# Gathering a sample's compression rows in two halves, and compressing its keys and values side by side

## The chip, the cores and the metric

The kernel runs on one core of one Trainium2 chip. The time of a run is the device time of that core in microseconds (us), from one launch; the median of three runs is the figure that counts. An "engine" is one of the core's five instruction streams: PE (matrix multiply; its weight loads are listed apart as PEld), DVE (vector), ACT (scalar and activation), POOL (general, and here the issuer of indirect DMAs) and SP (which only issues DMAs).

## The reference, cut to what matters

One decoder layer is computed for two request groups: a prompt of 1024 tokens, and 8 samples of 8 new tokens each, with 2048 tokens of past in paged caches.

```
x = ffn_half(x, norm_ffn1, ffn1_wg, ffn1_wu, ffn1_wd)     # x + (silu(h@wg) * (h@wu)) @ wd / 2
q, kc, vc, ks, vs, kw, vw, gates, z, xbc, dtr = split_proj(rmsnorm(x) @ w_in)
o_att  = nsa_mixer(q, ...)      # compressed, selected and window attention
y_ssm  = mamba_mixer(z, xbc, ...)
x = x + concat(o_att, y_ssm) @ w_out
x = ffn_half(x, norm_ffn2, ffn2_wg, ffn2_wu, ffn2_wd)

def compress(rows, pe, w1, w2):            # once for K, once for V
    ch  = rows.reshape(b, T // 16, 16, KV_HEADS, HEAD_DIM)
    blk = concatenate([ch[:, :-1], ch[:, 1:]], axis=2) + pe      # blocks of 32 tokens, stride 16
    blk = blk.transpose(0, 1, 3, 2, 4).reshape(b, nc - 1, KV_HEADS, 32 * HEAD_DIM)
    return silu(blk @ w1) @ w2
```

The change touches `compress` for the samples' past only: for each of 8 samples, 128 chunks of 16 tokens are fetched from the paged cache and turned into 127 compressed keys and 127 compressed values for each of 2 KV heads.

## The kernel before, in words

All of the kernel is one program whose order on each engine is fixed when it is built (a scheduler works on a model of the engines and writes out one list per engine). The tokens, 1024 of the prompt and 64 of the samples, make 1088 columns, worked on as two halves of 544, each cut into pieces of 256 and of 288 columns (`SUBS`). Nearly every product in fp32 is made of three passes, a high part and a low part of each operand: weights-high times data-high, weights-low times data-high, weights-high times data-low. On the page these show as three lines one after another: L366, L367, L368 for gate and up of the feed-forward parts (outputs gX and gY), L412 to L414 for the first columns of it (output g), L633 to L635 for the down projection (output dq), L250 to L252 for the projections q, xbc, z. A weight load of 128x128 goes with each matmul.

The stages, in us from the span's start: gate and up of the first feed-forward part about 100 to 520, its down projection to 710, projections and Mamba to 1136, prompt attention to 1548, sample attention and output projection to 1760, gate and up of the second feed-forward part to 2170, its down projection to the end.

The moving operands of gate and up are the tiles B1 to B7 (`b_tiles`, L112), each of four k-slices of 256 or of 288 columns; the weights are `whi` and `wlo`. SBUF tiles come from stacked pools on two sides, "left" and "right" of the memory. The constants pool `C` (L214 for `idx`) is the first on the left, so its size sets where all later left-side tiles start. `b_tiles` puts filling tiles between the B tiles, so that these start at chosen bytes modulo 256 (`PLACE = (96, 160)`, L110).

In the attention stage the prompt's eight query tiles run one after another, and 3, 0, 2, 1, 1, 0, 1, 0 of the samples' compressions (`compress_sample`, L1702) are written ahead of them; the scheduler weaves the two together. One compression does this:

- one indirect DMA (`gather`, L1686, issued by POOL at L1689, with row numbers in `idx`) brings 128 chunks of 16 tokens into `chk`, one buffer of 16 KB per partition; the next gather can only be issued once every reader of that buffer is through,
- eight steps, four for K and then four for V. A step (`pairs`, L1704) copies 4 tokens' worth of rows into `chp` (half on ACT, half on POOL, L267), transposes it with four PE instructions into `cT` (L1712), and splits the result into `th` (ACT) and `tl` (DVE, L1717), of which there are two pairs. Twelve matmuls (L1733 to L1735) then add it to `cA` in PSUM; one step's `pairs` is written ahead of the step before's matmuls,
- after four steps, `cmp_hidden` (L1406) reads `cA` with ACT (L1410), and two small matmuls give the compressed keys, or values (`c2`).

`cA` is one PSUM buffer of half a bank, used by K, then by V, then by the next sample's K.

Of the kernel before, what the change touches and what calls it, by code (L numbers as in the profile page):

```python
# [10 lines left out]
F32 = mybir.dt.float32  # L11
F32R = mybir.dt.float32r
BF16 = mybir.dt.bfloat16
I32 = mybir.dt.int32
AF = mybir.ActivationFunctionType
OP = mybir.AluOpType
AX = mybir.AxisListType

P = 128
# [22 lines left out]
def f32(ap):  # L42
    return ap.bitcast(F32)
# [37 lines left out]
def hybrid_step(ctx: ExitStack, tc: tile.TileContext, *aps):  # L81
    nc = tc.nc
# [129 lines left out]
    w2 = C.tile([P, 2, 64], F32, name="w2")  # L212
    gd = C.tile([P, 9, 32], F32, name="gd")
    idx = C.tile([P, 8], I32, name="idx")  # L214


    def blocks(n):
# [48 lines left out]
    def copy(eng, out, src):  # L266
        return nc.scalar.copy(out, src) if eng == "a" else ENGINES[eng].tensor_copy(out, src)  # L267
# [448 lines left out]
    def late():  # L716
        at = 0
        for name, n in VECS:
            nc.sync.dma_start(vr[at:at + n], rows(A[name], n))
            at += n  # L720
        nc.sync.dma_start(w2[:, 0], A["cmp_w2_k"][0])
        nc.sync.dma_start(w2[:, 1], A["cmp_w2_v"][0])

        ptile = C.tile([P, 8], I32, name="ptile")
        pt = A["page_table"]
        for a in range(16):
            nc.sync.dma_start(ptile[8 * a:8 * a + 8], bass.AP(
                tensor=pt.tensor, offset=pt.offset + a, ap=[[0, 8], [16, 8]]))
        nc.vector.tensor_scalar(w2, w2, 0.5, None, op0=OP.mult)
        q = bankx("vec_ps")  # L730
        nc.tensor.transpose(q[:, :NV], vr, ident[:NV, :NV])
        nc.vector.tensor_copy(vec, q[:, :NV])
        lane = C.tile([P, 1], I32, name="lane")
        nc.gpsimd.iota(lane, pattern=[[0, 1]], base=0, channel_multiplier=1)
        nc.vector.tensor_scalar(lane, lane, 7, None, op0=OP.bitwise_and)
        lanef = C.tile([P, 1], F32, name="lanef")
        nc.vector.tensor_copy(lanef, lane)
        nc.vector.tensor_scalar(idx, ptile, 8.0, lanef, op0=OP.mult, op1=OP.add)

    def begin1():  # L740
        g = First(F1, w1g, silu_out, raw0)
# [932 lines left out]
    with pool("att", bufs=2) as K, pool("att_ps2", bufs=3, space=PSUM) as PS2, \  # L1674
# [3 lines left out]
            return PS1.tile([P, 512], F32, name=name, tag=tag, bufs=2 if name == "pT" else 1)  # L1678


        ch_cmp = A["cache_cmp"][0].rearrange("n (c s) k g d -> (n c) (s k g d)", s=16)
        with tc.issue_after(wload.ins):
            for b in range(8):
                nc.sync.dma_start(nwin_s[0, b, 0:504].rearrange("t k g d -> t (k g d)"),
                                  A["cache_win"][0, b, 8:512].rearrange("t k g d -> t (k g d)"))

        def gather(b):
            chk = CK.tile([P, 16, 2, 2, 64], F32, name="chk", bufs=1)
            nc.gpsimd.indirect_dma_start(  # L1689
                out=chk.rearrange("p s k g d -> p (s k g d)"), out_offset=None, in_=ch_cmp,  # L1690
                in_offset=bass.IndirectOffsetOnAxis(ap=idx[:, b:b + 1], axis=0))
            return chk

        first_chk = gather(0)

        tpad = []
        for i in range(2):
# [2 lines left out]
                nc.gpsimd.memset(f32(t[:, :, 256:]), 0.0)  # L1700

        def compress_sample(b):  # L1702
            chk = gather(b) if b else first_chk
            def pairs(kv, jj):  # L1704
                chp = CK.tile([P, 2, 2, 2, 64], F32, name="chp", bufs=1)
                for g in range(2):
                    copy(KN["chp"][g], chp[:, :, g], chk[:, 4 * jj:4 * jj + 4, kv, g, :].rearrange(
                        "p (j r) d -> p j r d", r=2))
                q = b1("cT")
                for u in range(2):  # L1710
                    for g in range(2):
                        nc.tensor.transpose(q[:, P * (2 * u + g):P * (2 * u + g) + P],  # L1712
                                            chp[:, u, g].rearrange("p r d -> p (r d)"), ident)
                sv = q.rearrange("p (u c) -> p u c", u=2)
                th, tl = tpad[jj % 2]
                copy(KN["th"][jj % 2], th[:, :, :256], sv)
                nc.vector.tensor_tensor(tl[:, :, :256], sv, f32(th[:, :, :256]), op=OP.subtract)  # L1717

            steps = [(kv, jj) for kv in range(2) for jj in range(4)]
            pairs(*steps[0])  # L1720
            for kv in range(2):
                ab = PSC.tile([P, 2, P], F32, name="cA")
                for jj in range(4):
                    if (kv, jj) != steps[-1]:
                        pairs(*steps[4 * kv + jj + 1])
                    th, tl = tpad[jj % 2]
                    for u in range(2):
                        j = 2 * jj + u
                        for z in range(2):
                            wh, wl = w1h[:, kv, 8 * z + j], w1l[:, kv, 8 * z + j]  # L1730
                            first = j == 0 and z == 0
                            mh, ml = (x[:, u, z:z + 256].rearrange("p (g c) -> p g c", g=2) for x in (th, tl))
                            nc.tensor.matmul(ab, wh, mh, start=first, stop=False, skip_group_check=True)  # L1733
                            nc.tensor.matmul(ab, wl, mh, start=False, stop=False, skip_group_check=True)
                            nc.tensor.matmul(ab, wh, ml, start=False, stop=(j == 7 and z == 1), skip_group_check=True)  # L1735
                hs = cmp_hidden(CK, ab[:, :, :127], None, kv, 127)
                q = b1("c2")
                for g in range(2):
                    if kv == 0:
# [793 lines left out]
```

## Time and profile before

| what | value |
|---|---|
| median of 3 runs | 2473.76 us (2468.87 to 2475.54) |
| the profiled execution's own time | 2475.45 us |
| its span, first to last instruction | 2473.8 us |
| mean granted TensorE clock | 0.987 |
| PE busy | 2408.8 us, 97% of the span |
| PE weight loads | 2222.8 us, 90% |
| DVE / ACT / POOL busy | 71% / 46% / 17% |
| bytes moved by DMA | 379.07 MB, mean 153 GB/s |

"Busy" adds up the time during which an engine has at least one instruction at work; consecutive matmuls overlap, so how long a matmul really takes of the engine is read from the distance between the starts of two of them, not from the length of one. "Idle before" is time in which an engine stood still ahead of an instruction, with the instruction that released it.

### The profile page before, as it was taken

What the parts mean: (1) busy time and instruction counts of PE and PEld (TensorE: products, weight loads), DVE (VectorE), ACT (ScalarE), POOL (GpSimd) and SP (SyncE); (2) the same over time, 40 slices, a digit from 0 to 9 for tenths busy, and PEclk for the clock granted to TensorE, in tenths of its full rate; (3) what the DMA queues carried; (4) which work ended last, traced back from release to release, by engine and by line L of the source; (5) the groups of instructions that cost most, each with busy time, mean ns of one, the idle gap of its engine ahead of it and who ended that gap; (6) DMA issues with size and microseconds to landing.
All of it is one profiled execution on the core that took longest, in us unless ns stands there. A gap on an engine that the chain in (4) does not pass through costs nothing.

```text
span 2473.8 us, 48193 instructions
## 1 busy us (share of the span) xinstructions
PE 2408.8 (97%) x19026; PEld 2222.8 (90%) x19026; DVE 1744.7 (71%) x3673; ACT 1131.2 (46%) x2501; POOL 418.3 (17%) x533
## 2 busy tenths in 40 slices
PE   7999999999999999999999999999999999999998
PEld 6999999999999998997667766677899999999998
DVE  6777776677778855655656666777967676768776
ACT  7544444441133254425666675444545454543113
POOL 0000000011134343333434343111000000001110
PEclk9999999999999999999999998999999999999999
DMA  4334343598652333423110104476235353559654
GB/s 162 134 133 160 130 164 129 175 338 306 230 190 84 126 116 102 119 69 127 40 64 35 69 35 148 130 250 213 89 123 171 120 174 120 174 213 370 238 209 153
DMA packets 230446, 379.07 MB, mean 153 GB/s; under 512 B 18509, under 2 KB 147705, under 8 KB 228812
## 3 DMA queue, kind: packets, MB, share of 16 engines
q1 hardware_dynamic: 210248, 318.02, 37.7%
q0 software_dynamic: 7600, 38.59, 4.5%
q10 hardware_dynamic: 12372, 19.38, 2.2%
q8 instruction: 150, 2.46, 0.4%
q14 instruction: 76, 0.62, 0.1%
HBM read 255.66 MB, written 124.40 MB: 154 GB/s over the span
## 4 chain that ended last, share of the span: by engine, by line
PE 86%; DVE 6%; DMA 4%; ACT 3%; issue 1%; POOL 0%; ACTq 0%; DVEq 0%; POOLq 0%
PE dq L634 6%; PE gY L367 6%; PE dq L633 6%; PE dq L635 6%; PE gY L368 6%; PE gY L366 6%; PE gX L367 5%; PE gX L366 5%; PE gX L368 5%; PE o L1855 3%; PE pT L1846 3%; PE s L1808 1%; PE xbc L250 1%; PE xbc L251 1%; PE xbc L252 1%; PE cA L1733 1%
## 5 line engine op out<-in xcount | busy, mean ns | idle before, releaser
L634 PE MATMUL dq<-db,da 128*128 128x256 f32 (+1 forms) x1232 | 353.2, 288 | 0.3 <-DVE da L270 0.3
L635 PE MATMUL dq<-db,da 128*128 128x256 f32 (+1 forms) x1232 | 352.8, 288 | 0.0
L633 PE MATMUL dq<-db,da 128*128 128x256 f32 (+1 forms) x1232 | 349.8, 288 | 2.7 <-DVE Cc L386 2.2
L642 DVE TENSOR_TENSOR xT<-xT,dq 128x256 f32<-128x256 f32 (+1 forms) x456 | 186.9, 432 | 84.8 <-PE dq L635 83.2
L270 POOL TENSOR_TENSOR ds<-dw 128x512 f32<-128x512 f32 x22 | 29.5, 1341 | 1228.1 <-DVE wlo L270 508.0
L633 PEld LDWEIGHTS dq<-db,da 128*128 128x128 f32 x1232 | 230.5, 189 | 3.3 <-DVE Cc L386 2.5
L635 PEld LDWEIGHTS dq<-db,da 128*128 128x128 f32 x1232 | 232.8, 189 | 0.0
L634 PEld LDWEIGHTS dq<-db,da 128*128 128x128 f32 x1232 | 231.9, 188 | 0.6 <-DVE da L270 0.5
L267 ACT CAST whi<-ws 128x512 fp32r<-128x512 f32 x156 | 96.5, 623 | 205.9 <-PE gY L368 137.6
L270 DVE TENSOR_TENSOR wlo<-raw,whi 128x512 fp32r<-128x512 f32 x184 | 125.5, 687 | 83.9 <-ACT whi L267 83.5
L267 ACT CAST da<-ds 128x512 fp32r<-128x512 f32 x88 | 52.6, 623 | 234.7 <-PE dq L635 93.4
L267 ACT CAST whi<-raw 128x512 fp32r<-128x512 f32 x181 | 112.4, 626 | 72.0 <-PE g L414 19.5
L270 DVE TENSOR_TENSOR wlo<-ws,whi 128x512 fp32r<-128x512 f32 x156 | 106.7, 687 | 42.4 <-ACT whi L267 41.9
L1824 ACT ACTIVATE pb<-s,mx 128x256 f32<-128x256 f32 (+3 forms) x192 | 105.0, 552 | 59.7 <-DVE mx L1822 37.6
L1846 PEld LDWEIGHTS pT<-ident,pb 128*128 128x128 f32 x528 | 59.6, 143 | 45.8 <-issue 40.1
L1821 DVE TENSOR_REDUCE mx<-s 128x1 f32<-128x384 f32 (+2 forms) x128 | 66.6, 536 | 44.0 <-PE s L1813 34.1
L366 PE MATMUL gY<-B3h,whi 128*128 128x256 f32 (+1 forms) x320 | 91.5, 287 | 1.5 <-ACT whi L267 1.4
L366 PE MATMUL gX<-B6h,whi 128*128 128x256 f32 (+1 forms) x320 | 91.3, 286 | 0.9 <-ACT Cc L373 0.9
L367 PE MATMUL gX<-B6h,wlo 128*128 128x256 f32 (+1 forms) x320 | 91.4, 286 | 0.6 <-DVE wlo L270 0.6
L367 PE MATMUL gY<-B3h,wlo 128*128 128x256 f32 (+1 forms) x320 | 91.6, 287 | 0.2 <-DVE wlo L270 0.2
L277 POOL TENSOR_TENSOR pb<-pb,sm 128x640 f32<-128x640 f32 (+7 forms) x70 | 85.1, 1238 | 37.6 <-DVE sm L1831 34.0
L367 PE MATMUL gY<-B2h,wlo 128*128 128x256 f32 (+1 forms) x320 | 91.4, 286 | 0.0
(763 smaller groups left out, 8548.1 us busy)
## 6 DMA issues: line engine op xcount, KB each, us to landing
db<-GD SPq DMA_DIRECT2D x42, 1632.0 KB
GD<-Cc SPq DMA_DIRECT2D x154, 272.0 KB
GD<-his SPq DMA_DIRECT2D x84, 272.0 KB
raw<-in_ffn_wu_dram SPq DMA_DIRECT2D x22, 1024.0 KB
dw<-in_ffn_wd_dram SPq DMA_DIRECT2D x44, 512.0 KB
raw<-in_ffn_wg_dram SPq DMA_DIRECT2D x21, 1024.0 KB
GD<-hp SPq DMA_DIRECT2D x70, 272.0 KB
db<-GD SPq DMA_DIRECT2D x14, 1088.0 KB
```

What stands on the lines that cost most here:

```text
L267: return nc.scalar.copy(out, src) if eng == "a" else ENGINES[eng].tensor_copy(out, src)
L270: ENGINES[eng].tensor_tensor(out, x, y, op=op)
L277: nc.gpsimd.tensor_tensor(out, x, by.to_broadcast(list(x.shape)), op=OP.mult)
L366: nc.tensor.matmul(q, ah[:, k], b_, start=first, stop=False, skip_group_check=True)
L367: nc.tensor.matmul(q, al[:, k], b_, start=False, stop=False, skip_group_check=True)
L368: nc.tensor.matmul(q, ah[:, k], c_, start=False, stop=(k == 3), skip_group_check=True)
L633: nc.tensor.matmul(q, x, bh[:, u, o], start=first, stop=False, skip_group_check=True)
L634: nc.tensor.matmul(q, y, bh[:, u, o], start=False, stop=False, skip_group_check=True)
L635: nc.tensor.matmul(q, x, bl[:, u, o], start=False, stop=(u == np_ - 1), skip_group_check=True)
L642: nc.vector.tensor_tensor(x, x, q, op=OP.subtract if i == 4 else OP.add)
L1824: nc.scalar.activation(pb[:, st:st + pn], s, AF.Exp, bias=mx[:, 0:1], accum_out=part[:, hh_, i:i + 1])
L1846: nc.tensor.transpose(tq_[:kn, P * hh_:P * hh_ + P], src, ident)
```

## The change

The cache is viewed as chunks of 8 tokens, not 16, and each sample's rows come in two gathers of 8 KB per partition into two buffers. A second table of row numbers, `idx2`, is made from `idx` (2·idx and 2·idx + 1): 64 bytes per partition in the constants pool and two DVE instructions early in the program. Both halves of sample 0 are asked for at the start; a half of the next sample is asked for inside `compress_sample`, behind the fourth and the eighth `pairs`. The eight steps go K, V, K, V, ...: step n does tokens of quarter n // 2 for K (n even) or V (n odd). `cA` now holds K and V together and takes a whole bank; its matmuls have one start for the pair. `cmp_hidden` and `c2` for K and for V come after all eight steps.

```
     idx = C.tile([P, 8], I32, name="idx")
+    idx2 = C.tile([P, 2, 8], I32, name="idx2")
...
         nc.vector.tensor_scalar(idx, ptile, 8.0, lanef, op0=OP.mult, op1=OP.add)
+        for u in range(2):
+            nc.vector.tensor_scalar(idx2[:, u], idx, 2.0, float(u), op0=OP.mult, op1=OP.add)
...
-        ch_cmp = A["cache_cmp"][0].rearrange("n (c s) k g d -> (n c) (s k g d)", s=16)
+        ch_cmp = A["cache_cmp"][0].rearrange("n (c s) k g d -> (n c) (s k g d)", s=8)
...
-        def gather(b):
-            chk = CK.tile([P, 16, 2, 2, 64], F32, name="chk", bufs=1)
+        def gather(b, u):
+            chk = CK.tile([P, 8, 2, 2, 64], F32, name="chk", bufs=2)
...
-                in_offset=bass.IndirectOffsetOnAxis(ap=idx[:, b:b + 1], axis=0))
+                in_offset=bass.IndirectOffsetOnAxis(ap=idx2[:, u, b:b + 1], axis=0))
...
-        first_chk = gather(0)
+        chks = [gather(0, 0), gather(0, 1)]
...
-            chk = gather(b) if b else first_chk
-            def pairs(kv, jj):
+            def pairs(n):
+                jj, kv = n // 2, n % 2
+                chk = chks[jj // 2]
...
-                th, tl = tpad[jj % 2]
+                th, tl = tpad[n % 2]
...
+                if n % 4 == 3 and b < 7:
+                    chks[jj // 2] = gather(b + 1, jj // 2)
-            steps = [(kv, jj) for kv in range(2) for jj in range(4)]
-            pairs(*steps[0])
+            pairs(0)
+            abs_ = PSC.tile([P, 2, 2, P], F32, name="cA")
+            for n in range(8):
+                jj, kv = n // 2, n % 2
+                ab = abs_[:, kv]
+                if n < 7:
+                    pairs(n + 1)
...
+                        first = n == u == z == 0
...
             for kv in range(2):
-                ab = PSC.tile([P, 2, P], F32, name="cA")
...
-                hs = cmp_hidden(CK, ab[:, :, :127], None, kv, 127)
+                hs = cmp_hidden(CK, abs_[:, kv, :, :127], None, kv, 127)
```

The built programs differ in two ways: in order within the attention stage, and in where tiles lie.

**Order.** The first place is POOL's list at the start of the attention stage, where `QB` and `QA` are operands of the scores, and `pc`, `pb` are softmax weights that POOL scales. Before, ahead of the first `chp` copy:

```order
L1700 MEMSET tl_13758 128x2x2
L1637 MEMSET QB_13182 1x128 x2
L270 TENSOR_TENSOR pc<-pc,sm 128x512
L1637 MEMSET QB_13182 1x128
L277 TENSOR_TENSOR pb_14384<-pb_14384,sm 128x384
L277 TENSOR_TENSOR pb_14392<-pb_14392,sm 128x384
L277 TENSOR_TENSOR pb_14400<-pb_14400,sm 128x384
L1637 MEMSET QB_13182 1x128
L267 CAST QA<-QA 64x2x128
L270 TENSOR_TENSOR QB_13184<-qT,QA 64x2x128
L267 COPY chp<-chk 128x2x128
```

The same place now (line numbers are higher by 1 to 7 from here on, and the numbers behind names are different):

```order
L1703 MEMSET tl_13763 128x2x2
L1640 MEMSET QB_13185 1x128
L268 COPY chp<-chk 128x2x128
L1640 MEMSET QB_13185 1x128
L271 TENSOR_TENSOR pc<-pc,sm 128x512
L1640 MEMSET QB_13185 1x128
L278 TENSOR_TENSOR pb_14394<-pb_14394,sm 128x384
L278 TENSOR_TENSOR pb_14402<-pb_14402,sm 128x384
L278 TENSOR_TENSOR pb_14410<-pb_14410,sm 128x384
L268 COPY chp<-chk 128x2x128
```

The first copy out of the gathered rows has moved ahead of the scaling of `pc` and of three `pb`. Somewhat later on the same engine the first half of sample 1 is asked for, where before the whole buffer had to be free first:

```order
L268 CAST QA<-QA 64x2x128
L271 TENSOR_TENSOR QB_13188<-qT,QA 64x2x128
L1692 DMA chk<-in_cache_cmp_dram,idx_182 128x2048
L278 TENSOR_TENSOR pb_14581<-pb_14581,sm 128x384
L278 TENSOR_TENSOR pb_14589<-pb_14589,sm 128x384
L268 COPY chp<-chk 128x2x128 x4
L1692 DMA chk<-in_cache_cmp_dram,idx_182 128x2048
```

There are now 16 such issues, where there were 8.

The second place is PE's list where the first compression step's matmuls stand among the prompt's scores (`s`), transposes (`pT`) and outputs (`o`). Before:

```order
L1808 MATMUL s_14580<-KA,QA 128x384
L1810 MATMUL s_14580<-KB,QB_13183 128x384
L1813 LDWEIGHTS identb
L1813 MATMUL s_14580<-mdiag,identb 128x128
L1733 MATMUL cA<-th_13753,w1h 128x256
L1734 MATMUL cA<-th_13753,w1l 128x256
L1855 MATMUL o<-pt,VA 64x512 x2
```

Now:

```order
L1716 MATMUL cT<-ident,chp 128x128 x3
L1815 MATMUL s_14450<-KA,QA 128x384
L1817 MATMUL s_14450<-KB,QB_13185 128x384
L1820 LDWEIGHTS identb
L1820 MATMUL s_14450<-mdiag,identb 128x128
L1815 MATMUL s_14527<-KA,QA 128x384
L1817 MATMUL s_14527<-KB,QB_13186 128x384
L1820 LDWEIGHTS identb
L1820 MATMUL s_14527<-mdiag,identb 128x128
L1853 MATMUL pT<-ident,pb_14386 128x128 x2
L1739 MATMUL cA<-th_13758,w1h 128x256
L1740 MATMUL cA<-th_13758,w1l 128x256
```

The first `cA` matmul has moved ahead of scores and transposes behind which it stood. PE has as many matmuls as before. Outside the attention stage, PE's list is the same up to a handful of swaps of neighbours.

**Places in SBUF.** The 64 bytes of `idx2` move every left-side tile that is opened after the constants by 64 bytes per partition; right-side tiles and PSUM tiles stay where they were. Of the big matmuls, these are the start bytes modulo 256 in the two built programs ("alternating" is over the four k-slices, since 288 columns of 4 bytes are 1152 bytes):

| matmuls | before: moving / weights | now: moving / weights |
|---|---|---|
| first gate and up, 256 columns | 96 / 160 | 96 / 224 |
| first gate and up, 288 columns | 32 and 160 alternating / 160 | 32 and 160 alternating / 224 |
| second gate and up, 256 columns | 160 / 224 | 224 / 224 |
| second gate and up, 288 columns | 96 and 224 alternating / 224 | the same |
| down, 256 and 288 columns | 224 (L633, L634), 96 (L635) / 224 | the same |
| q, xbc, z, 256 and 288 columns | 96 and 224 alternating / 224 | the same |

More of the change, by code (lines that the diff above doesn't have):

```diff
@@ L1702, in compress_sample @@
         def compress_sample(b):
-            chk = gather(b) if b else first_chk
-            def pairs(kv, jj):
+            def pairs(n):
+                jj, kv = n // 2, n % 2
+                chk = chks[jj // 2]
                 chp = CK.tile([P, 2, 2, 2, 64], F32, name="chp", bufs=1)
                 for g in range(2):
-                    copy(KN["chp"][g], chp[:, :, g], chk[:, 4 * jj:4 * jj + 4, kv, g, :].rearrange(
+                    copy(KN["chp"][g], chp[:, :, g], chk[:, 4 * (jj % 2):4 * (jj % 2) + 4, kv, g, :].rearrange(
                         "p (j r) d -> p j r d", r=2))
@@ L1714, in pairs @@
                 sv = q.rearrange("p (u c) -> p u c", u=2)
-                th, tl = tpad[jj % 2]
-                copy(KN["th"][jj % 2], th[:, :, :256], sv)
+                th, tl = tpad[n % 2]
+                copy(KN["th"][n % 2], th[:, :, :256], sv)
                 nc.vector.tensor_tensor(tl[:, :, :256], sv, f32(th[:, :, :256]), op=OP.subtract)
-            steps = [(kv, jj) for kv in range(2) for jj in range(4)]
-            pairs(*steps[0])
-            for kv in range(2):
-                ab = PSC.tile([P, 2, P], F32, name="cA")
[L1723 to L1735, printed above, removed]
-                hs = cmp_hidden(CK, ab[:, :, :127], None, kv, 127)
@@ new lines, in pairs @@
+                if n % 4 == 3 and b < 7:
[7 more added lines that the diff above has]
+                    pairs(n + 1)
+                th, tl = tpad[n % 2]
+                for u in range(2):
+                    j = 2 * jj + u
+                    for z in range(2):
+                        wh, wl = w1h[:, kv, 8 * z + j], w1l[:, kv, 8 * z + j]
+                        first = n == u == z == 0
+                        mh, ml = (x[:, u, z:z + 256].rearrange("p (g c) -> p g c", g=2) for x in (th, tl))
+                        nc.tensor.matmul(ab, wh, mh, start=first, stop=False, skip_group_check=True)
+                        nc.tensor.matmul(ab, wl, mh, start=False, stop=False, skip_group_check=True)
+                        nc.tensor.matmul(ab, wh, ml, start=False, stop=(j == 7 and z == 1), skip_group_check=True)
```

## The prediction

> **What bounds the kernel now.** I read first the busy time of each engine, then the shares of the chain of waits, then busy time stage by stage.
>
> ```profile
> PE 2408.8 (97%) x19026; PEld 2222.8 (90%) x19026; DVE 1744.7 (71%) x3673; ACT 1131.2 (46%) x2501; POOL 418.3 (17%) x533
> PE 86%; DVE 6%; DMA 4%; ACT 3%; issue 1%; POOL 0%; ACTq 0%; DVEq 0%; POOLq 0%
> core 0: us, PE busy (x) PEld busy (x) DVE busy (x) ACT busy (x) POOL busy (x), PEclk, DMA share, GB/s
> 100.00:520.00 420.00, 416.77 (x3355) 415.91 (x3354) 298.89 (x513) 197.17 (x396) 1.29 (x1) 1.00 0.46 157
> ...
> 1136.00:1548.00 412.00, 399.87 (x2663) 287.23 (x2662) 264.46 (x638) 265.76 (x717) 159.45 (x237) 0.98 0.19 68
> 1760.00:2170.00 410.00, 409.76 (x3317) 409.07 (x3316) 296.44 (x530) 195.27 (x394) 0.00 (x0) 1.00 0.40 135
> 2180.00:2470.00 290.00, 281.42 (x2258) 280.24 (x2256) 219.57 (x460) 89.82 (x194) 29.24 (x22) 0.99 0.67 245
> ```
>
> PE is busy for 97% of the span and holds 86% of the chain. In the attention stage, which the change rewrites, PE stands still for 412.00 − 399.87 = 12.1 us in all; in the two gate and up stages it stands still for 3.2 and 0.2 us. So two things can move the end: how many of those 12.1 us the new gathers and the new order take away or add to, and how fast a matmul follows another. The second isn't a matter of waits, and is what the shift of tiles by 64 bytes can touch.
>
> For it I look at how far apart the starts of back-to-back matmuls lie. Four stretches, each with the first row, the next of another width, and so on:
>
> ```profile
> 299.84 0.28 PE L366 MATMUL gX<-B1h,whi 128*128 128x256 f32 x1
> ...
> 301.21 0.29 PE L366 MATMUL gX<-B1h,whi 128*128 128x288 f32 x1
> ...
> 302.80 0.28 PE L366 MATMUL gY<-B2h,whi 128*128 128x256 f32 x1
> ...
> 1990.75 0.28 PE L366 MATMUL gY<-B3h,whi 128*128 128x256 f32 x1
> ...
> 1992.13 0.28 PE L367 MATMUL gX<-B1h,wlo 128*128 128x256 f32 x1
> ...
> 640.97 0.28 PE L633 MATMUL dq<-db,da 128*128 128x256 f32 x1
> ...
> 642.03 0.29 PE L633 MATMUL dq<-db,da 128*128 128x288 f32 x1
> ...
> 643.21 0.28 PE L633 MATMUL dq<-db,da 128*128 128x256 f32 x1
> 1115.44 0.28 PE L250 MATMUL q<-hh,whi 128*128 128x256 f32 x1
> ...
> 1116.85 0.40 PE L250 MATMUL q<-hh,whi 128*128 128x256 f32 x2
> ```
>
> Between rows lie 12, 12, 12, 9, 9 and 12 matmuls. That gives for 256 columns 1.37/12 = **114.2 ns** in the first gate and up, 1.38/12 = **115.0 ns** in the second, 1.06/9 = **117.8 ns** in the down projection and 1.41/12 = **117.5 ns** in q; and for 288 columns 1.59/12 = 132.5 ns in gate and up, 1.18/9 = 131.1 ns in down. Same engine, same three-pass loop, same clock of 1.00; what differs is the table of start bytes above. Take the distance from moving operand to weights modulo 128: it is 64 for the 256 columns of both gate and up stages, and 0 for everything else in that table. Per column, 114.2/256 = 0.446 ns at distance 64, and 117.8/256 and 132.5/288, both 0.460 ns, at distance 0. The lengths by shape say it over all matmuls:
>
> ```profile
> L368 PE MATMUL gX<-B1l,whi 128*128 128x256 f32 x160 | 44.3, 277 | 0.0
> L634 PE MATMUL dq<-db,da 128*128 128x256 f32 x616 | 172.6, 280 | 0.3 <-DVE da L270 0.3
> L368 PE MATMUL gY<-B4l,whi 128*128 128x288 f32 x160 | 47.2, 295 | 0.0
> ```
>
> All 21 such rows of gate and up with 256 columns lie at 276 to 279 ns, the three of dq at 280 to 281. The three or so ns are small, but not noise: the groups don't overlap. That the start bytes are the cause is my reading; no row here varies them alone.
>
> **The change, part by part.**
>
> *Tiles shifted by 64 bytes, 256 columns.* Now both gate and up stages have distance 0 modulo 128 for 256 columns, like the down projection. The matmuls are 21 rows of 160 and 12 rows (L412 to L414) of 32, in both stages together 3744, 1872 in each. First stage: 117.8 − 114.2 = 3.6 ns, times 1872 = 6.7 us. Second: 117.8 − 115.0 = 2.8 ns, times 1872 = 5.2 us. Nothing hides it, since PE stands still for only 3.2 us in the one stage and 0.2 in the other. Sum **+12.0 us**; with q's 117.5 it is 10.9, so 11 to 13.
>
> *The same, 288 columns of the first stage.* Their 1872 matmuls go from distance 0 to 64, and modulo 256 half of them to the 64 below, as the fast 256 columns have it, and half to the 64 above, which no row shows. No row shows 288 columns at any distance but 0. If the cost goes by the column, they gain 132.5 − 0.446·288 = 4.0 ns each, −7.5 us; the same size up, +7.5 us, is the other bound. The nearest rows of the same width, in gate and up and down, all lie at 131 to 133 ns whatever the line, and I take **0**. This is the choice on which the forecast hangs most.
>
> *Gathers in halves, two buffers.* What the gather costs now:
>
> ```profile
> L267 POOL COPY chp<-chk x64: 388/398/428, 1149.7 to 1504.2; 128x256 f32<-128x256 f32 x64
> L1689 POOL DMA_INDIRECT chk<-in_cache_cmp_dram,idx x8: 1012/1013/1062, 1133.1 to 1453.4; - x8
>   DMA chk<-in_cache_cmp_dram,idx: 23.9, 12
>   ACT chp L267: 3.4, 3
>   PEld cT L1712: 2.5, 3
>   PEld o L1855: 0.8, 1
>   PE cT L1712: 0.3, 1
> 1147.96 0.40 ACT L267 COPY chp<-chk 128x256 f32<-128x256 f32 x1 [0.78 <-DMA chk<-in_cache_cmp_dram,idx]
> ```
>
> The copies out of `chk` stood waiting for a landing for 23.9 us in 12 places, but PE and its weight loads waited for those copies for only 2.5 + 0.8 + 0.3 = 3.6 us. The rest was covered by the prompt's scores and outputs, which PE works on in between. So two buffers can gain 3.6 us at the most. Of the first sample's wait little goes: its gather is issued at the same point, and PE now comes to the first `cT` ahead of three scores that stood before it; it may wait there instead. I take **−1.5 us**, less than half.
>
> On the other side stand 8 more issues of 1.01 us on POOL, 8.1 us. POOL is busy for 159.45 of the 412 us, so there is room, but POOL works in order: behind an issue that waits for the last reader of its half stand the next `chp` copies and the scaling of `pb`, for which PE's transposes wait. Before, such a wait for ACT's copy came in 3 issues, 3.4 us, so 1.13 us each. At the worst, every one of the 14 issues inside the loop waits that long, 14 · 1.13 + 8.1 = 24 us of POOL; with the share of time in which POOL is busy, 0.39, as the share that comes through to PE, 9.3 us. So −3.6 to +9.3, and I stay near the first, since its rows are PE's own waits.
>
> *K and V side by side, one bank of `cA`.* PE has the same matmuls. The wait that is added: the first `cA` matmul of a sample now waits for both `cmp_hidden` of the sample before, and behind it on PE stand scores and outputs.
>
> ```profile
>   ACT pb L1824: 4.1, 5
>   ACT th L267: 4.0, 6
> ```
>
> Of the first `cA` line's waits (L1733) these two are the longest, and the reading of `cA` by ACT is not among them, though the buffer already changed hands 16 times through that reading. It now does so 8 times. I take 0; the bounds are in the 9.3 us above and 4.0 us, were all of the waits for `th` gone. Where the order is new, waits of the prompt's work move about; with 12.1 us of still time in the whole stage this is the same scale again.
>
> *The second table of rows.*
>
> ```profile
> L738 DVE TENSOR_SCALAR idx<-ptile,lanef x1: 225/225/225, 44.1 to 44.1; 128x8 int32<-128x8 int32 x1
> ```
>
> Two more of these are 0.45 us of DVE at 44 us, ahead of a stage in which DVE works 298.89 of 420 us. I take 0; bare, it would be +0.45.
>
> *Sum.* 12.0 + 0 − 1.5 + 0 + 0 = **+10.5 us**. The profiled execution took 2475.45 us (span 2473.8), so it would be 2486.0. The median of the runs shown is 1.69 us below that execution; put on the median, 2473.76 + 10.5 = **2484.3 us**.
>
> [...]
>
> **The rivals.**
>
> *The shift costs nothing* (ends on the other side, not slower). The difference of 3 ns belongs to the loops, not to the start bytes: gate and up and down also differ in output tiles and in where the weights come from. For it: no row changes start bytes alone, and `cA`, with other patterns, isn't as clear. Against it: 256 and 288 columns of the very same lines differ per column, 0.446 and 0.460. It decides from a slope of less than 0.6 ns a matmul, where the 256 columns cost 3744 · 0.6 = 2.2 us. The sum is then −1.5, **2472.3 us**, and down to 2466 if all 3.6 us of the copies and all 4.0 us of the `th` waits go, as −7.6 us.
>
> *The 288 columns gain as the 256 lose.* For it: both widths have 0.460 ns a column at distance 0. Then 12.0 − 7.5 − 1.5 = +3.0, **2476.8 us**.
>
> *The 288 columns lose again.* For it: half of them come to a distance that the fast ones don't have, and any placing may be worse than the present one. Then 12.0 + 7.5 − 1.5 = +18.0, **2491.8 us**.
>
> *New waits on POOL.* Half of the 9.3 us above comes through: 12.0 + 4.7 = +16.7, **2490.5 us**.
>
> **How the numbers follow.** Chances: forecast 0.40, shift costs nothing 0.20, 288 columns gain 0.18, lose 0.17, new waits on POOL 0.05. About 0.3%, 7.4 us, is what a measurement of this kernel can tell from no change, so the bounds are 2466.3 and 2481.2. Slower: forecast, loss and POOL, 0.40 + 0.17 + 0.05 = 0.62. The first rival and the gain, 0.38, lie within, but for 0.05 of the first which with all of the gather's gains passes the lower bound: same 0.33, faster 0.05. The range takes in the forecast, the gain, the loss and most of the first rival: 2471 to 2492 us.
>
> **What would show it.** The spacing of 256-column matmuls in both gate and up stages: about 117 to 118 ns and a length of 280 ns if the first term holds, 114 to 115 and 277 if not; the two stages then take 6.7 and 5.2 us longer, far away from any edited line. The spacing of 288 columns in the first stage, beside the same in the second, whose places don't change: 132.5 in both by the forecast, 128.5 or 136.5 in the first by the two rivals. In the attention stage: PE's still time, 12.1 us now, at about 10.5; waits for `chk` among PE's, 3.6 us now, near 0; the wait of an issue for ACT's or its own copies well under 16 us in sum. I would be wrong if the gate and up stages take the same time as before while the attention stage changes by more than 8 us, or if the dense spacing changes in stages whose places didn't move.

## The result, and the profile after

The change makes the kernel slower: 2503.66 us, the median of 4 runs (2499.97 to 2505.49), against 2471.8 us before (4 runs, 2468.87 to 2475.54). The ratio is 1.0127 with a 95% interval of 1.0113 to 1.0141, so +31.9 us, three times the forecast and outside the range.

From the page of the changed kernel, and the busy times of the attention stage from its first score to its last output, before and then after (busy PE, PEld, DVE, ACT and POOL, then granted clock, DMA share and GB/s):

```profile
span 2501.3 us, 48212 instructions
PE 2431.7 (97%) x19026; PEld 2246.3 (90%) x19026; DVE 1754.2 (70%) x3675; ACT 1135.4 (45%) x2501; POOL 426.2 (17%) x541
...
1138.30:1547.40 409.10, 396.96 (x2641) 284.81 (x2640) 264.00 (x637) 265.76 (x716) 159.31 (x235) 0.98 0.18 67
...
1142.70:1566.70 424.00, 406.73 (x2642) 293.72 (x2641) 274.02 (x637) 268.56 (x716) 167.15 (x242) 0.95 0.18 62
```

The number of matmuls is the same, and still PE is busy for 23 us longer. In the attention stage the granted clock is 0.95, where it was 0.98. PE stands still there for 17.3 us, where it was 12.1, and is busy for some 9.7 us longer. The span of the profiled execution grew by 27.5 us, in these places:

| stage | before, us | after, us | difference |
|---|---|---|---|
| first gate and up | 491.2 | 496.7 | +5.5 |
| first down | 234.7 | 234.7 | 0 |
| projections, Mamba | 394.3 | 393.1 | −1.2 |
| prompt attention with the compressions | 409.1 | 423.9 | **+14.8** |
| sample attention, output projection | 206.1 | 206.4 | +0.3 |
| second gate and up | 470.0 | 477.9 | +7.9 |
| second down | 237.7 | 237.7 | 0 |

**Gate and up.** These are rows of the timeline of PE after; between two neighbours lie 12 matmuls of 288, 256, 288 and 256 columns in turn.

```profile
300.38 0.30 PE L367 MATMUL gY<-B3h,whi 128*128 128x288 f32 x1
...
301.97 0.29 PE L368 MATMUL gY<-B4h,wlo 128*128 128x288 f32 x1
...
306.02 0.28 PE L367 MATMUL gY<-B2h,whi 128*128 128x256 f32 x1
...
307.44 0.29 PE L367 MATMUL gY<-B2h,whi 128*128 128x288 f32 x1
...
1999.97 0.30 PE L367 MATMUL gY<-B2h,whi 128*128 128x288 f32 x1
...
2001.56 0.28 PE L367 MATMUL gX<-B6h,whi 128*128 128x256 f32 x1
...
2002.99 0.30 PE L367 MATMUL gX<-B6h,whi 128*128 128x288 f32 x1
```

Only differences within a stretch count. 301.97 − 300.38 = 1.59, so 132.5 ns with 288 columns as before; 307.44 − 306.02 = 1.42, so 118.3 ns with 256 in the first stage; 1.59 and 1.43 in the second, so 132.5 and 119.2 ns. Over all matmuls of the trace the means with 256 columns are 114.5 before and 118.3 after in the first stage, 114.2 and 119.5 in the second, and the distances that were recorded add up to 6.8 and 8.5 us more. (These sums leave out some of the distances, so they are a little under the full count.) The rows by shape show the same: L368 with gX and 256 columns had a length of 277 ns, and now, one line number higher,

```profile
L369 PE MATMUL gX<-B1l,whi 128*128 128x256 f32 x160 | 45.1, 282 | 0.0
...
L635 PE MATMUL dq<-db,da 128*128 128x256 f32 x616 | 172.6, 280 | 0.3 <-DVE da L271 0.3
```

dq, whose tiles didn't move, is where it was, at 280 ns.

**The gathers** do what they are meant to do for the copies. The first row is what the readers of `chk` waited for, the others are who waited for its copies, after:

```profile
  DMA chk<-in_cache_cmp_dram,idx: 3.5, 2
...
  PEld cT L1716: 1.3, 1
  PE cT L1716: 1.1, 1
  PEld cA L1739: 0.8, 1
```

The copies wait for a landing for 3.5 us instead of 23.9, and PE and its weight loads wait for the copies for 3.2 us in all instead of 3.6. So next to nothing of the 3.6 us was gained: PE now waits at the first sample's first transposes, for 1.14 us at 1149.91 us, as the prediction had said that it might.

**Where PE waits in the attention stage**, the longest waits by line, before and then after, with total, times and the longest (`s` are scores, `c` the small matmuls that read the hidden part `cxh`):

```profile
PE s L1808 <- ACT pb L1824: 3.8, 10, 0.7
...
PE c L1743 <- DVE cxh L1414: 1.1, 2, 0.6
...
PE s L1815 <- ACT pb L1831: 5.3, 7, 2.6
PE c L1750 <- DVE cxh L1417: 3.3, 2, 2.1
PE c L1747 <- DVE cxh L1417: 1.2, 1, 1.2
```

The scores' wait grew from 3.8 to 5.3 us and that of the small matmuls from 1.1 to 4.5, and there are single waits of 1.2 to 2.6 us now. The wait of 2.11 us has a plain course: `cxh` is one buffer, so V's hidden part can't be written before K's small matmuls have read it. They start at 1306.16 us, ACT begins V's part at 1307.20, DVE ends it at 1309.57, and V's small matmuls start at 1309.71. Before, V's four steps lay between the two.

What comes behind such a wait is in the clock column. "Half speed" stands for a stretch in which the trace shows a granted clock of 0.5. These windows are the 3.4 us in which PE's wait of 2.58 us for `pb` began and those in which its wait of 2.11 us for `cxh` began (2.0 and 1.1 us of still time lie inside), each with the 6.8 us behind it:

```profile
1271.20:1274.60 3.40, 1.36 (x12) 1.16 (x11) 3.36 (x6) 0.50 (x3) 3.26 (x5) 1.00 0.28 116
1274.60:1281.40 6.80, 6.26 (x28) 5.37 (x28) 2.49 (x6) 2.77 (x9) 0.70 (x3) 0.50 0.00 0
...
1305.30:1308.70 3.40, 2.30 (x12) 0.97 (x11) 1.78 (x7) 2.73 (x8) 0.20 (x1) 1.00 0.00 0
1308.70:1315.50 6.80, 5.79 (x26) 5.11 (x27) 3.17 (x10) 3.98 (x11) 5.78 (x6) 0.50 0.00 0
```

PE was busy for 1.36 and 2.30 of 3.4 us, and was then granted half speed for 6.8 us. In the stage as a whole the trace after has 44.4 us at half speed, 40.4 of them busy, and before 17.1, all busy. How much such a stretch costs shows where the same matmuls run on from one into full clock: in the trace after, those of xbc with 256 columns (L251 to L253) start 213.5 ns apart at half speed (754.39 to 758.66 us, 20 steps) and 118.3 ns at full clock (761.35 to 763.48 us, 18 steps), so 45% of the time at half speed is lost there; one half is taken here as a round estimate. Half of the difference in busy time, 11.7 us, is somewhat more than the 9.7 us by which PE is busy longer; the other 5 or so of the stage's +14.8 are time in which it stands still.

### The profile page after: what moved, and what is told of

Read it like the earlier page. It is cut to its first block, busy times and chain, and to the rows that moved or that the text cites. A ratio compares the mean times of both kernels' runs of the same rounds, so it can differ in the third digit from the quotient of the medians.

```text
span 2501.3 us, 48212 instructions
## 1 busy us (share of the span) xinstructions
PE 2431.7 (97%) x19026; PEld 2246.3 (90%) x19026; DVE 1754.2 (70%) x3675; ACT 1135.4 (45%) x2501; POOL 426.2 (17%) x541
## 4 chain that ended last, share of the span: by engine, by line
PE 87%; DVE 5%; ACT 3%; DMA 2%; issue 1%; POOL 0%; ACTq 0%; SPq 0%; DVEq 0%; POOLq 0%
PE gY L368 6%; PE gY L369 6%; PE gY L367 6%; PE dq L635 6%; PE dq L636 6%; PE dq L634 6%; PE gX L368 5%; PE gX L369 5%; PE gX L367 5%; PE o L1862 3%; PE pT L1853 3%; PE s L1815 1%; PE cA L1739 1%; PE s L1817 1%; PE xbc L251 1%
## 5 line engine op out<-in xcount | busy, mean ns | idle before, releaser
L635 PE MATMUL dq<-db,da 128*128 128x256 f32 (+1 forms) x1232 | 353.4, 288 | 0.3 <-DVE da L271 0.3
L634 PE MATMUL dq<-db,da 128*128 128x256 f32 (+1 forms) x1232 | 349.6, 288 | 2.5 <-DVE Cc L387 2.1
L634 PEld LDWEIGHTS dq<-db,da 128*128 128x128 f32 x1232 | 230.5, 189 | 3.2 <-DVE Cc L387 2.4
L635 PEld LDWEIGHTS dq<-db,da 128*128 128x128 f32 x1232 | 231.9, 188 | 0.6 <-DVE da L271 0.5
L268 ACT CAST da<-ds 128x512 fp32r<-128x512 f32 x88 | 52.6, 623 | 234.7 <-PE dq L636 93.4
L268 ACT CAST whi<-raw 128x512 fp32r<-128x512 f32 x181 | 112.4, 625 | 74.6 <-PE gY L369 19.4
L1828 DVE TENSOR_REDUCE mx<-s 128x1 f32<-128x384 f32 (+2 forms) x128 | 67.3, 536 | 44.4 <-PE s L1820 38.2
L368 PE MATMUL gX<-B6h,wlo 128*128 128x256 f32 (+1 forms) x320 | 92.3, 289 | 0.6 <-DVE wlo L271 0.6
L368 PE MATMUL gY<-B3h,wlo 128*128 128x256 f32 (+1 forms) x320 | 92.3, 289 | 0.2 <-DVE wlo L271 0.2
L368 PE MATMUL gX<-B7h,wlo 128*128 128x256 f32 (+1 forms) x320 | 92.4, 289 | 0.0
L369 PE MATMUL gY<-B2l,whi 128*128 128x256 f32 (+1 forms) x320 | 92.4, 289 | 0.0
L369 PE MATMUL gY<-B3l,whi 128*128 128x256 f32 (+1 forms) x320 | 92.3, 289 | 0.0
```

The costliest lines, as they stand in the source:

```text
L368: nc.tensor.matmul(q, al[:, k], b_, start=False, stop=False, skip_group_check=True)
L369: nc.tensor.matmul(q, ah[:, k], c_, start=False, stop=(k == 3), skip_group_check=True)
L634: nc.tensor.matmul(q, x, bh[:, u, o], start=first, stop=False, skip_group_check=True)
L635: nc.tensor.matmul(q, y, bh[:, u, o], start=False, stop=False, skip_group_check=True)
```

## The experiments

Twelve kernels were run, each beside runs of the kernel before on the same chip. Every trace is of a single execution, not always one near the median. Two theories stood at the start: that the loss has two causes, the places of the tiles (in gate and up) and the new order (in attention), against one cause, either the places or the 16 gathers.

**e1_shift64**: the shift without the change.

```
     idx = C.tile([P, 8], I32, name="idx")
+    C.tile([P, 16], I32, name="spare")
```

> The kernel before with nothing but 64 unused bytes in the constants pool, so that the left-side tiles lie where the change puts them. Two-causes theory (places of tiles cost in gate and up, the new order costs in the attention stage): +13 to +17 us against before, gate and up spacings for 256 columns of 118 to 120 ns, attention stage unchanged within 3 us. Places-alone theory (all of the loss of the change is the shift): about +32 us, the attention stage longer by 15. If the spacing belongs to the loops and not to the places: within 3 us of before.

Measured: 2487.38 us against 2470.88, ratio 1.0055 (1.0035 to 1.0076). PE's order is that of before, instruction for instruction. The means with 256 columns are 118.3 and 119.5 ns, those of the changed kernel to the tenth, and the stages of gate and up 499.0 and 478.2 us. The attention stage took 404.4, 4.7 us less than before and not within the 3 us expected, with 10.2 us at half speed instead of 17.1. So the places of the left-side tiles make this part, and it isn't all of the loss.

**e2_after_in_place**: the change without the shift; both tables of row numbers lie in tiles that were there.

```
-    idx2 = C.tile([P, 2, 8], I32, name="idx2")
+    idx2 = []
...
-        for u in range(2):
-            nc.vector.tensor_scalar(idx2[:, u], idx, 2.0, float(u), op0=OP.mult, op1=OP.add)
+        nc.vector.tensor_scalar(ptile, idx, 2.0, 0.0, op0=OP.mult, op1=OP.add)
+        nc.vector.tensor_scalar(idx, idx, 2.0, 1.0, op0=OP.mult, op1=OP.add)
+        idx2.extend((ptile, idx))
...
```

> The change with both tables of row numbers in tiles that were there already, so that no tile moves; PE has the order of the change. Two-causes theory: +14 to +19 us against before (2503.7 less about 15), spacings of gate and up back at 114 to 115 ns, attention stage as long as in the change. Places-alone theory: as before, within 3 us.

Measured: 2495.84 us against 2470.88, ratio 1.0089 (1.0069 to 1.0109): 25.0 us, more than expected. 256 columns are back at 114.5 and 114.3 ns; the attention stage takes 423.6 us, with 37.5 us at half speed. The trace is of the longest of the four runs, 2504.26 us. PE's order and its long waits (2.6 for `pb`, 2.1 for `cxh`) are those of the change.

**e3_side_by_side** and **e4_halves**: the two parts of the change in `compress_sample`, one each, without a shift. e3 has the alternating steps, the one bank and the late hidden parts with one gather as before; e4 has the two gathers, with keys and then values:

```
+                chk = chks[jj // 2]
...
+                if kv and jj % 2 and b < 7:
+                    chks[jj // 2] = gather(b + 1, jj // 2)
```

> The kernel before with one part of the change alone: keys and values step by step side by side, in one bank, with both hidden parts after the eighth step; one gather of 16 tokens into one buffer as before, no tile moved. Theory that the side-by-side order makes the loss of the attention stage (PE waits for the hidden parts at the end of each sample, and the clock drops behind these waits): +10 to +18 us. Theory that the 16 gathers on POOL make it: within 4 us of before.

> The other part alone: halves of 8 tokens into two buffers, asked for behind the second and the fourth step of the values, with keys and then values as before, no tile moved. Side-by-side theory: within 3 us of before. Gather theory: +10 to +18 us.

Measured: e3 2494.18 us, ratio 1.0085 (1.0056 to 1.0114), 23.3 us and again more than expected; e4 2475.16 us, ratio 1.0015 (1.0002 to 1.0027), 4.3 us where at most 3 were expected. The attention stage takes 427.3 us in e3 (47.8 at half speed) and 407.5 in e4 (13.7). The loss of the stage belongs to the order of the steps, and next to none of it to the gathers.

**e5_free_change** and **e6_free_before**: what if PE waits for no hidden part? In e2 and in before, the small matmuls that make the compressed keys and values read weights.

```
-                        nc.tensor.matmul(q[64 * g:64 * g + 64, :127], w2[:, 0], hs[:, g, :127],
+                        nc.tensor.matmul(q[64 * g:64 * g + 64, :127], w2[:, 0], f32(w1h[:, 0, g])[:, :127],
...
```

> The side-by-side order of e2 (no tile moved), but the small matmuls that make the compressed keys and values read weights that have long been there instead of the hidden part, so that PE waits for no hidden part; ACT and DVE still compute it. What the compressed keys and values of the samples are made from is thereby another thing. Theory that the waits for the hidden parts at the end of each sample cost the attention stage its 15 to 18 us (by themselves and by the clock that drops behind them): stage at 406 to 413 us, +0 to +5 us against before in all. Theory that the weaving of the new steps with the prompt's work costs it (waits for softmax weights, queries and splits): stage at 418 us or more, +12 us or more.

> The same edit in the kernel before, as a control: the compressed keys and values of the samples are made from weights. Both theories: within 4 us of before, since PE waited for the hidden part there for little more than 1 us; a clear change here would say that the edit itself moves the order enough to matter, and e5 is then read against it.

Measured: e5 2492.36 us, ratio 1.0062 (1.0035 to 1.0089), e6 2479.95 us, ratio 1.0038 (1.0022 to 1.0053). In e5 no wait for `cxh` by the small matmuls is left, and still the stage takes 424.9 us with 41.0 at half speed (the five runs lie between 2479 and 2494 us, and the trace is of one at 2493.5): the scheduler wove the steps anew, and other waits came, these among the longest:

```profile
PE s L1816 <- ACT pb L1832: 7.4, 9, 2.4
PE cT L1717 <- ACT chp L268: 2.2, 1, 2.2
```

The control moved as well, by 8 us, twice the 4 us expected. Its stage takes 413.2 us with only 10.2 at half speed: there PE stands still for 17.2 us instead of 12.1, with longer waits of 1.7 us for `tl` and of 1.0 for `pb`. So the first theory of these waits missed: to take away the wait for `cxh` doesn't bring the time back. This edit can't say more, since it moves the order, and e6 shows that a new order can cost 8 us without any of the change.

**e7_k_first**: in e2, the keys' hidden part is written right behind the seventh step.

```
-            for kv in range(2):
-                hs = cmp_hidden(CK, abs_[:, kv, :, :127], None, kv, 127)
...
+                if n >= 6:
+                    finish(n - 6)
```

> The side-by-side order of e2 with the hidden part and the compressed keys written right behind the last step of K (the seventh), ahead of the last step of V; the values' as in the change. Theory of the waits for hidden parts: about half of the stage's loss goes, stage at 412 to 419 us, +5 to +14 us in all. Theory of the weaving: stage stays at 422 us or more, or moves either way.

Measured: 2486.29 us, ratio 1.0066 (1.0048 to 1.0085), 9.5 us below e2 by the medians. The intervals of the ratios overlap, though the highest run of e7, 2489.88 us, lies below the lowest of e2, 2492.24. The stage takes 412.5 us with 13.7 at half speed, in the shortest of e7's runs (2482.57), so the 11 us between the two traces overstate what the edit does.

**e11_late_hidden** is its counterpart: the kernel before, steps K and then V, and only the hidden parts both at the end.

```
+            abs_ = PSC.tile([P, 2, 2, P], F32, name="cA")
             for kv in range(2):
-                ab = PSC.tile([P, 2, P], F32, name="cA")
+                ab = abs_[:, kv]
...
-                hs = cmp_hidden(CK, ab[:, :, :127], None, kv, 127)
+            for kv in range(2):
+                hs = cmp_hidden(CK, abs_[:, kv, :, :127], None, kv, 127)
```

> The kernel before with keys and then values as they were, one gather, no tile moved, but K and V in one bank and both hidden parts behind the eighth step, as in the change: the late hidden part alone, without the alternation of steps. Theory that the late hidden part costs the stage its time (in e7, alternating, writing K's hidden part earlier brought the stage to 412.5 us): stage at 417 us or more, +9 us or more in all. Theory that it is the alternation: stage at 412 us or less, within 4 us of before.

Measured: 2486.47 us against 2471.82, ratio 1.0053 (1.0032 to 1.0073). The stage takes 414.3 us with 23.9 at half speed, between the two expectations; the total sides with the late hidden part. Four long waits of e11 (1.67, 1.12, 2.09 and 1.68 us) stand at the same points as in e3 (1.68, 1.12, 2.09 and 1.91 us there). Two of them, in the timeline of PE with the wait in brackets:

```profile
1198.57 0.44 PE L1742 MATMUL c<-cxh,w 128*64 128x127 f32 x4 [1.67 <-DVE cxh L1414]
...
1426.91 0.44 PE L1742 MATMUL c<-cxh,w 128*64 128x127 f32 x4 [2.09 <-DVE mx L1824]
```

So the late hidden part alone brings these waits without any alternation; e3 has two more, of 1.74 us for `pt` and 2.47 us for `pb`. But the same wait of 2.09 us was followed by 13.7 us at half speed in e3, and by 6.8 us in e11. The intervals of e3 and e11 overlap, and how much of e3's larger loss is the alternation, and how much such luck, stays open.

**e9_filler** puts the question to the clock. In e2, eight useless matmuls stand between the last step of each sample and the wait for its hidden part.

```
                 q = b1("c2")
+                if kv == 0:
+                    for _ in range(8):
+                        nc.tensor.matmul(q[:, 256:512], w1h[:, 0, 0], w1h[:, 0, 0:2], start=True, stop=True,
+                                         skip_group_check=True)
```

> The side-by-side order of e2 (no tile moved) with eight useless matmuls of 256 columns between the last step of each sample and the wait for its hidden part, 64 in all, 64 x 0.118 = 7.5 us of PE at full clock, into a part of PSUM that nobody reads. Clock theory (most of the loss of the attention stage is half speed in a fixed window of 3.4 us after one in which PE was busy for less than about 0.6): clock time lost in the stage falls from 18.8 us to below 14, and the stage is no longer than in e2 (423.6 us) in spite of the added work, +18 to +26 us in all. Waits alone (the clock is a by-product): stage at 427 us or more, clock time lost unchanged, +27 us or more.

Measured: 2489.16 us against 2471.72, ratio 1.0081 (1.0065 to 1.0097), 6.7 us below e2 by the medians though their intervals overlap. The busy times of the stage, e2 and then e9, each between its first score and its last output:

```profile
1147.70:1571.30 423.60, 404.30 (x2640) 290.79 (x2640) 274.13 (x637) 268.60 (x716) 167.15 (x242) 0.96 0.18 63
```

```profile
1137.80:1556.90 419.10, 402.29 (x2705) 293.56 (x2704) 269.17 (x637) 268.03 (x716) 167.43 (x242) 0.98 0.18 62
```

64 matmuls more, and the stage is 4.5 us shorter, with 17.1 us at half speed instead of 37.5 (e2's trace is of its longest run, as said). The waits of 2.6 us for `pb` and 2.1 for `cxh` are gone, and PE stands still for 16.8 us instead of 19.3. But the order moved as well: about 680 of the stage's 2639 matmuls stand elsewhere, when the change itself moved about 790 of before. So it isn't the clock by itself that was varied. Fewer long waits go with less half speed here; that the filler did it, and not the new order, is not shown.

**e8_shift128, e10_da_place, e12_da_160** test the rule of the prediction, with PE's order as before (in all three, and in e1, matmul for matmul). e8 has 128 unused bytes in the constants pool, where e1 has 64. e10 and e12 move the weights of the down projections by tiles of 192 or 64 bytes ahead of them, with the rest to 256 behind:

```
-        Ds_, "right", "da0 da1 dw000 dw100 dw010 dw110 db0 db1 ds10 ds20 ds11 ds21"))
+        Ds_, "right", "sa0 da0 da1 sb0 dw000 dw100 dw010 dw110 db0 db1 ds10 ds20 ds11 ds21"))
...
```

> The kernel before with 128 unused bytes in the constants pool instead of 64. If the distance between moving operand and weights modulo 128 sets the spacing, both gate and up stages have 64 again with 256 columns and 0 with 288: spacings of 114 to 115 and 132 to 133 ns, total within 4 us of before. If any move away from the chosen places costs, or the distance counts modulo 256: +7 us or more, spacings of 117 ns or more.

> The kernel before with the weights of both down projections (da) moved by unused bytes so that they start at 32 instead of 224 modulo 256; the order on every engine is that of before. Rule from the runs so far: with 256 columns the fast spacing comes where the moving operand starts 64 below the weights modulo 256, and with no other distance of 0, 64 and 128 tried. L633 and L634 with 256 columns (1232 matmuls) come to that distance: 114 to 115 ns instead of 117.3, -3.7 us; L635 (616) goes from 128 below to 64 above, unchanged; 288 columns unchanged within 0.7 ns. In all -2 to -5 us, which 5 rounds may or may not tell from nothing; the spacings decide. If the fast spacing belongs to the gate and up loops alone: spacings unchanged.

> As e10, but the weights of the down projections start at 160: L635 with 256 columns then has the very pair of start bytes, 96 and 160, that goes with 114.5 ns in the first gate and up. If the pair of start bytes sets the spacing: L635 at 114 to 115 ns, L633 and L634 (224 and 160) at 117 to 118. If the loops have a part in it: L635 at 117 or more, as with 224 and 32. In all within 4 us of before in both cases; the spacings decide.

Measured: e8 2483.11 us, ratio 1.0044 (1.0027 to 1.0061); e10 2473.08 us, ratio 1.0006 (0.9994 to 1.0017); e12 2473.69 us, ratio 1.0006 (0.9995 to 1.0017). The means with 256 columns, over all pairs of start bytes that were run:

| matmuls | moving / weights | mean ns |
|---|---|---|
| first gate and up, before / e1 / e8 | 96/160, 96/224, 96/32 | 114.5 / 118.3 / 117.6 |
| second gate and up, before / e1 / e8 | 160/224, 224/224, 32/224 | 114.2 / 119.5 / 117.6 |
| down L633, before / e10 / e12 | 224/224, 224/32, 224/160 | 117.2 / 117.3 / 118.0 |
| down L634, before / e10 / e12 | 224/224, 224/32, 224/160 | 117.4 / 116.9 / 118.5 |
| down L635, before / e10 / e12 | 96/224, 96/32, 96/160 | 117.4 / 118.5 / 116.6 |

In e8 the distance modulo 128 is 64 again, and the spacing isn't fast. Modulo 256, what was fast has the moving operand 64 below the weights; but in the down projection that distance gives 117.3, 116.9 (e10) and 116.6 (e12), though L635 of e12 has the very pair 96/160. Places mattered here, by 3.1 to 5.3 ns in gate and up, and no rule from this kernel says which are good. In gate and up all left-side tiles move at once, so these runs don't tell whether it is PE's reading of its two operands that counts or what other engines and DMAs touch beside it; e10 and e12, which move `da` and little else, change the spacing by no more than 1.1 ns.

**The clock over all traces.** The stage from its first score to its last output, the time at half speed within it, and the time in which PE stands still:

| kernel | PE's order in the stage | stage, us | at half speed | stage less half of that | PE still |
|---|---|---|---|---|---|
| before, e1, e8, e10, e12 | before | 409.1, 404.4, 404.6, 406.1, 403.9 | 17.1, 10.2, 10.2, 13.7, 6.8 | 400.6, 399.3, 399.5, 399.3, 400.5 | 12.1, 11.8, 12.8, 12.0, 12.3 |
| after, e2 | change | 423.9, 423.6 | 44.4, 37.5 | 401.7, 404.9 | 17.3, 19.3 |
| e9 | change with 7.5 us of filler | 419.1 | 17.1 | 410.5 | 16.8 |
| e3 | side by side | 427.3 | 47.8 | 403.4 | 18.6 |
| e5 | change, `cxh` not read | 424.9 | 41.0 | 404.4 | 19.4 |
| e11 | late hidden part | 414.3 | 23.9 | 402.4 | 16.0 |
| e7 | side by side, K's hidden part early | 412.5 | 13.7 | 405.7 | 15.9 |
| e6 | before, `cxh` not read | 413.2 | 10.2 | 408.1 | 17.2 |
| e4 | halves | 407.5 | 13.7 | 400.6 | 14.1 |

Five kernels with one and the same order of PE differ by 5.2 us, and by 1.3 us once half of their time at half speed is taken off. PE's busy time says the same for all orders: it goes from 391.7 to 408.7 us, and without half of what lies at half speed it is 385 to 391 us in every trace but e9's, whose filler adds 7.5. In the order of the change PE stands still for 5 to 7 us more than in the order of before; the rest of the stage's loss is busy time, and that is mostly the clock. In e6, against the trace of before, it is the still time alone that grew.

Every kernel with another order than before's has more still time, whatever the edit. So that any new weaving of these steps does worse than the one of before is a rival to the late hidden parts that these runs don't exclude. Nor was the late hidden part run with a second buffer for `cxh`, which would let V's part be written beside K's.

## Why the prediction was wrong

**Where the chain stands**: right. PE bounds the kernel, and the gathers' landing was off its path. The wait of an issue for the copies is 4.5 us in sum, well under the 16 us named. PE's wait for the copies, forecast near 0, is 3.2 us. The gathers' term was −1.5 us with bounds of −3.6 and +9.3; e4, the halves without the rest, measured 1.0002 to 1.0027, which is +0.5 to +6.7 us on 2470.88: inside the bounds, though not the gain that was chosen; the 4.7 us of the rival of new waits on POOL lie inside that interval too.

**256 columns, +12.0 us**: right in its kind, too small in size. The term was taken at the spacing of the down projection, 117.8 ns; the moved tiles came to 118.3 and 119.5. The 115.0 ns for the second stage, from one stretch, was too high as well: the mean over that stage is 114.2. From the means, (118.3 − 114.5) · 1872 = 7.1 us and (119.5 − 114.2) · 1872 = 9.9 us, 17.0 in all; the recorded distances add up to 15.3. e1, with only the shift, measured 1.0055 (1.0035 to 1.0076). The rival by which the shift costs nothing is thereby out: 114.2 against 119.5 ns with the same instructions in the same order.

The reading behind the term, a distance modulo 128, was wrong all the same, as e8 shows. It gave the right sign for this shift by luck, since both new pairs, 96/224 and 224/224, are slow; it would have promised no loss for a shift by 128, which costs 1.0027 to 1.0061.

**288 columns, 0**: right. 133.0 and 132.1 ns before, 132.2 and 131.9 after for the two starts of the first stage, some 0.5 ns, or 0.9 us in all.

**Side by side, 0**: this step failed; it is where most of the loss lies, 23.3 us in e3 and 25.0 in e2. The text said that "PE has the same matmuls" and took the added waits as nothing, with 12.1 us of still time as the scale of them. Two things were wrong. The first is the wait itself: PE's still time was forecast at about 10.5 us and came to 17.3. The second is that the waits here had a price beyond their length, and this is the larger part: PE is busy for 9.7 us longer in the stage, with 44.4 us at half speed instead of 17.1. The clock stood in the rows of before (0.98 in the stage's window, 17.1 us at half speed in its trace), and the prediction quoted that column and didn't use it. With it, the question would have been whether the new order puts waits of over 1 us at places where there had been none. The diff showed such a place: both hidden parts, a chain over ACT and DVE through one buffer of `cxh`, now stand right behind the last step, where before V's four steps lay behind K's sums and covered K's chain. The prediction looked at who waits for `cA` and not at who waits for `cxh`.

e11 and e7 speak for this from both sides: late hidden parts alone cost 1.0032 to 1.0073, and K's hidden part written early takes 9.5 us off e2 by the medians. e5 and e6 set the limit: with the wait for `cxh` gone, e5's stage is as long as that of the change, with other waits of 2.2 and 2.4 us, and the control loses 8 us. That the order of the steps makes the loss is shown by e2, e3 and e4; which of its waits make it is only in part.

The parts don't add up to the whole by their medians: 16.5 (e1) and 25.0 (e2) against 31.9 us. By their intervals, 8.6 to 18.8 and 17.1 to 26.9, the two can add up to it. The trace after has 5.5 + 7.9 us in gate and up and 14.8 in attention, of 27.5.

## What to carry to other kernels

Price a wait on TensorE not only by its length: find in the profile how many of the waits are followed by a reduced clock (in the attention stage 17.3 us of still time went with 44.4 us at half speed after, 12.1 with 17.1 before), and ask of every new order whether it gathers PE's idle time into waits of over 1 us, as the chain over ACT and DVE at the end of an accumulation did here, with waits of up to 2.1 us for `cxh`, the one buffer that two such chains share. Have a control that moves the order without the change, since a new order alone cost 8 us here. Before a small tile is put ahead of everything else in SBUF, compare the start bytes of the operands of the matmuls that take most of the time (64 bytes took their spacing from 114.5 to 118.3 and from 114.2 to 119.5 ns in e1); keep them by reusing a tile or by filling up, and measure, since no rule seen here carried from one loop to another. A latency that PE's own rows didn't show waiting for was worth next to nothing here, however long the copies waited: their wait for a landing fell from 23.9 to 3.5 us, and PE's for the copies from 3.6 to 3.2.

## What the runs showed of the hardware

In these traces the clock was granted in steps of 3.413 us (every stretch at half speed is a multiple of it, from 3.41 to 23.89 us, but for the one that runs past the program's end), and the steps stand at another point of the program from trace to trace: one begins 72.69 us after the span's start in the trace of before, and one 73.09 us after it in that of the change. Over the 14 traces, between 100 and 2450 us: after a step at full clock in which PE was busy for under 0.45 of it, half speed followed in 40 of 41 cases; between 0.45 and 0.75 in 66 of 177; above it in 29 of some 9190. These counts show no sharp bound at the 0.6 of e9's clock theory. In the attention stage of the trace after, half speed set in seven times. The longest wait of PE that began in the step before was 2.58 us (for `pb`), 2.11, 1.18 and 1.14 (for `cxh`) and 1.02 (for `pc`) in five of them, and shorter in two. The same wait was followed by more or less of it: one of 1.0 us at the start of the stage by none in the trace of before, by 3.4 us at half speed in e12 and by 6.8 in e10, with one and the same order. So one profile is one draw: the attention stage with the order of before took 403.9 to 409.1 us in five of them.

Where tiles start in SBUF changed the spacing of 256-column fp32 matmuls by up to 5.3 ns (114.2 before, 119.5 in e1, second gate and up), and that of 288 columns by less: means of 132.0 to 133.1 ns in the two stages of gate and up, over before, e1 and e8, and 131.7 to 133.9 in L635 of the down projection, over before, e10 and e12.
